# Moving the modulation sums of two output projections to other stages of a two-block network

## The chip, the cores and the metric

One core of a Trainium2 chip. The time is device microseconds of one execution, the median of several runs. The core has five engines that run side by side, each through its own instructions in order: TensorE (PE, with its weight loads as PEld), VectorE (DVE), ScalarE (ACT), GpSimd (POOL) and SyncE (SP), which here issues nearly all DMA transfers.

## The reference, cut to what matters

Two transformer-like blocks run one after the other on x of 1024 tokens by 1024 channels, all in float32. Each block is modulated by six vectors that come from a conditioning vector through a 1024 by 6144 matrix:

```python
mod = (silu(c) @ w_mod + b_mod)                  # block 1; block 2: silu(c_2) @ ada_w + ada_b
sh1, sc1, g1, sh2, sc2, g2 = split(mod, 6)
h = rms(x, norm1_w) * (1 + sc1) + sh1            # block 1's mixers read this
x = x + g1 * (mixed @ w_out)                     # block 1's output projection
h2 = rms(x, norm2_w) * (1 + sc2) + sh2
x = x + g2 * conv_ffn(h2)                        # up projection, convolution, down projection
# block 2 alike, with layer norms and its own mixers; its gate g2 (part 5 of ada_w) is read by its last FFN stage
```

## The kernel before

The program is one class, `Net`; `run` calls the stages in order: `setup`, `block1_in`, `mixers`, `block1_out`, `block1_ffn` (an up stage and a down stage), `block2_in`, `block2_out`, `block2_ffn`. Matrix products are made of three PE passes over float32r halves (high by high, high by low, low by high), so every weight piece of 128x1024 that SP loads into one of two `wr` buffers is split by ACT (the high part) and by POOL or DVE in turn (the low part). In an output projection and a down stage a weight piece is first multiplied by the block's gate row on DVE (lines 134 and 1182).

A vector of the modulation is not a PE product but a sum over eight slabs of 128 rows of its weight: each slab is loaded, and each half (512 columns) is multiplied by the conditioning value of its partition and added to an accumulator. At the end PE adds over the partitions: with four matmuls for each half where a column layout is wanted (`mod_col`, line 208), or with one matmul to a single row (`mod_row`, line 227), to which DVE adds a bias row loaded by SP and which SP then stores to the tensor `gates` in DRAM.

Where these sums stand:
- block 1's `sh1` and `sc1`: in `block1_in`.
- block 1's gate 1 (`mod_gate1`): in `mixers`, whose work is ordered by the string `SSKKKSKKKKKQMSQQQQQAQAQGAAAAAA` (S: a quarter of the S5 layer, K: a tile of keys and values, Q: of queries, M: gate 1, A: attention, G: the gated linear unit). One half is summed by DVE alone (line 248), the other by ACT (product, line 242) and POOL (add, line 244). The slabs use the three buffers `sb`, of which the attention's bias setup holds one first, and the accumulators the two buffers `pp`, which the bias setup uses before.
- block 1's `sh2` and `sc2` (`MODS_OUT`) and block 2's gate of its FFN (`MODS_OUT2`): inside the two output projections, through `mods_out`, a generator from which `out_gemm` takes four steps after each of its first four tiles. A step is one slab of 512 KB into an `xn` buffer and two sums on DVE (lines 278 and 280). The `xn` and `hT` buffers are those of the norm that follows.
- the other sums: in block 1's up stage (`mods_up`) and down stage (`mods_down`), in steps of one half slab (256 KB into one of two `mw` buffers, one DVE sum, lines 299 and 301). The down stage takes three steps for each weight load: one behind the gate product, one behind each of two splits. `mods_end` turns the sums into columns and rows after tile 3 of the second column half, all through one PSUM bank.

The order of instructions on each engine is not the program's alone. A planner goes through the program with its own estimate of each instruction's time and puts on each engine, at each moment, the ready instruction that comes first in the program. What it estimates wrongly shows on the chip as a wait, because every engine's order is then fixed. `behind` only keeps a step's instructions from going ahead of a given one on the same engine.

`out_gemm` runs the projection of eight token tiles in two column halves: the first halves of tiles 0 to 3, their second halves, and then both halves of tiles 4 to 7. The weights of the second half are loaded after tile 1 of the first (`ws.append(load(1))`). `down_proj` runs two column halves over eleven weight loads each, with eight token tiles for each load.

Of the kernel before, what the change touches and what calls it, by code (L numbers as in the profile page):

```python
# [19 lines left out]
F32 = mybir.dt.float32  # L20
# [4 lines left out]
ALU = mybir.AluOpType  # L25
AX = mybir.AxisListType

P = 128
D = 1024
L = 1024  # L30
KT = D // P
# [5 lines left out]
ALPHA = 2.0 ** 0.25  # L37
# [28 lines left out]
class Net:  # L66
# [161 lines left out]
        nc.vector.tensor_add(b, b, ps)  # L228
        nc.sync.dma_start(self.gates[i:i + 1, sl], b)

    def mod_gate1(self, pool):

        nc = self.nc
        accs = [pool.tile([P, 512], F32, tag="pp", name="macc", bufs=2) for _ in range(2)]
        for k in range(KT):
            t = pool.tile([P, D], F32, tag="sb", name="mw", bufs=3)
            nc.sync.dma_start(t, self.a["w_mod"][k * P:(k + 1) * P, 2 * D:3 * D])
            s = self.cact[:, k:k + 1]
            for half, acc in enumerate(accs):
                th = t[:, half * 512:half * 512 + 512]  # L240
                if half:
                    nc.scalar.mul(th if k else acc, th, s)
                    if k:
                        nc.gpsimd.tensor_add(acc, acc, th)
                elif k == 0:
                    nc.vector.tensor_scalar(acc, th, s, None, op0=ALU.mult)
                else:
                    nc.vector.scalar_tensor_tensor(acc, th, s, acc, op0=ALU.mult, op1=ALU.add)
        for half, acc in enumerate(accs):
            self.mod_row(0, half, acc, "bm2", "m")  # L250


    MODS_OUT = [("w_mod", 3, [0], "sh2", "bm3"), ("w_mod", 4, [0], "sc2", "bm4")]
    MODS_UP = [("w_mod", 5, 0, 1, "bm5"), ("ada_w", 0, 1, "sh_a", "ab0"), ("ada_w", 0, 2, "sh_a", "ab0"),
               ("ada_w", 1, 1, "sc_a", "ab1"), ("ada_w", 1, 2, "sc_a", "ab1")]
    MODS_DOWN = [("ada_w", 2, 1, 2, "ab2"), ("ada_w", 3, 1, "sh_b", "ab3"), ("ada_w", 4, 1, "sc_b", "ab4")]
    MODS_OUT2 = [("ada_w", 5, [1], 3, "ab5")]

    def mod_put(self, to, half, acc, bias, vec, role):

        if isinstance(to, int):
# [1 line left out]
        else:  # L263
            self.mod_col(to + ("c" if vec == 2 else ""), half, acc, bias, role, plus_one=to.startswith("sc"),
                         gain="norm2" if to == "sc2" else None)

    def mods_out(self, pool, plan, role):

        nc, v = self.nc, self.nc.vector
        for w, part, (vec,), to, bias in plan:  # L270
            accs = [pool.tile([P, 512], F32, tag="hT", name="macc", bufs=2) for _ in range(2)]
            for k in range(KT):
                t = pool.tile([P, D], F32, tag="xn", name="xn", bufs=4)
                nc.sync.dma_start(t, self.a[w][k * P:(k + 1) * P, part * D:(part + 1) * D])
                for half, acc in enumerate(accs):
                    th, s = t[:, half * 512:half * 512 + 512], self.cact[:, vec * 8 + k:vec * 8 + k + 1]
                    if k == 0:
                        v.tensor_scalar(acc, th, s, None, op0=ALU.mult)
                    else:
                        v.scalar_tensor_tensor(acc, th, s, acc, op0=ALU.mult, op1=ALU.add)  # L280
                if k == KT - 1:
                    for half, acc in enumerate(accs):
                        self.mod_put(to, half, acc, bias, vec, role)
                yield

    def mod_half(self, w, part, vec, half, acc, pool):

# [390 lines left out]
    def mixers(self):  # L678

        nc, v, a = self.nc, self.nc.vector, self.a  # L680
        mq = self.mq
        t2 = lambda r: mq.tile([P, 512], F32, tag="q" + r, name="q" + r, bufs=2)
        self.attn_setup(mq)
        order = "SSKKKSKKKKKQMSQQQQQAQAQGAAAAAA"
        wk = wq = None
        kq = {c: 0 for c in "KQSMAG"}
        old, self.aT = self.aT, []
        qs, st = [], {}
        gl = ExitStack()

        def attend(s):
            if s < 2 * NT:
                self.attn_score(mq, s, qs, st)
            if 0 < s <= 2 * NT:
                self.attn_values(mq, t2, s - 1, st)
            if s > 2 and s % 2:
                self.attn_out(t2, (s - 3) // 2, st)

        ops = False
        for c in order:  # L700
            i = kq[c]
            kq[c] += 1
            if c == "K":
                wk = wk or [self.piece(a["w_kv"][k]) for k in range(2)]
                self.kv_tile(i, wk, t2, old)
            if c == "S":
                self.s5_quarter(i, self.tables)
                if i < 3:
                    self.tables = self.s5_tables(self.s5p, i + 1)
                else:  # L710
                    self.s5ctx.close()
            if c == "M":
                self.mod_gate1(mq)
            if c == "Q":
                wq = wq or [self.piece(a["w_q"][k]) for k in range(4)]
                qs.append(self.q_tile(i, wq, old, t2))
            if c == "A":
                if not ops:
                    ops = True
                    self.psum(1, o=1)  # L720
                if i % 4 == 0 and len(self.aT) == i // 4:
                    self.aT.append(self.new_act())
                attend(2 * i)
                attend(2 * i + 1)
            if c == "G":
                while len(self.aT) < 2:
                    self.aT.append(self.new_act())
                self.glu(self.pool(gl, "m1g", "right"))
        attend(2 * NT)
        attend(2 * NT + 1)  # L730
        gl.close()
        self.m1q.close()
# [210 lines left out]
                hi, lo = (t[:, m].rearrange("p (c t) -> p c t", t=8) for t in self.aT[n])  # L943
                self.split(hi, lo, zv)

    def out_gemm(self, pool, name, gate, xs_in, done, order, alpha=None, step=iter(()), act_in=None):

        nc, v = self.nc, self.nc.vector
        g = self.gate_row(gate)
# [12 lines left out]
        ws = [load(0)]  # L962

        for nh, i in [(0, 0), (0, 1), (0, 2), (0, 3), (1, 0), (1, 1), (1, 2), (1, 3), *((h, i) for i in range(4, NT) for h in (0, 1))]:
# [8 lines left out]
                v.scalar_tensor_tensor(xo, xo, alpha, ps, op0=ALU.mult, op1=ALU.add)  # L973
            if nh:
                done(i)
            elif i < 4:
                for _ in range(4):
                    next(step, None)
                if i == 1:
                    ws.append(load(1))  # L980

    def block1_out(self):
        nc, a = self.nc, self.a
# [21 lines left out]
        def turn(i):  # L1005
            if i % 4 == 0:
                new.append(self.new_act())
            if i % 2:
                self.transpose_mod(xn[i - 1:i + 1], new[-1], self.mods["sc2"], self.mods["sh2"], htile, i % 4 - 1, ("s5", "tp"))

        self.out_gemm(pool, "w_out", 0, lambda i: a["x"][i * P:(i + 1) * P], self.pipe(norm, turn),
                      (4, 5, 6, 7, 0, 1, 2, 3), step=self.mods_out(pool, self.MODS_OUT, "m"))
        self.aT = new
        es.close()

# [148 lines left out]
    def down_proj(self, down, gate, g_dr, x_dr, setup, done, slots, alpha, mods):  # L1164
# [12 lines left out]
        def load(nh, q):  # L1177
# [1 line left out]
            r = self.raw(self.a[down][nh * NQ + q])  # L1179
            w = [self.w.tile([P, 1024], F32R, tag=t, name=t, bufs=4) for t in ("wh", "wl")]  # L1180
            r2 = r.rearrange("p (k n) -> p k n", k=2)
            self.behind(v.tensor_tensor(r2, r2, gh, op=ALU.mult), step)
            self.split_on(nc.gpsimd, *w, r)
            hs = []
            for p in (2 * q, 2 * q + 1):
# [461 lines left out]
    def block2_out(self):  # L1647
# [27 lines left out]
        def turn(i):  # L1675
            if i % 4 == 0:
                new.append(self.new_act())
            if i % 2:
                self.transpose_mod(xn[i - 1:i + 1], new[-1], self.mods["sc_b"], self.mods["sh_b"], htile, i % 4 - 1)

        self.out_gemm(pool, "w_out2", 2, lambda i: None if i < 5 else self.x_dr[i], self.pipe(norm, norm2, turn), (6, 7, 4, 0, 1, 2, 5, 3), ALPHA,
                      self.mods_out(pool, self.MODS_OUT2, "tp"), mix_in)
        self.aT = new
        es.close()
        self.x5.close()
# [135 lines left out]
```

## Time and profile before

| | us |
|---|---|
| median of 3 runs | 2634.54 |
| lowest and highest run | 2631.08 and 2636.38 |
| the profiled execution | 2632.81 |
| its span, first to last instruction | 2630.4 |

The profile comes from that one execution. A busy share is the time in which an engine executed; the chain that ended last follows the end of the program back through what released each step; a wait is the idle time of an engine before an instruction, with the instruction or transfer that ended it. The granted clock is the share of TensorE's full clock in a stretch: 1.00 is 2.4 GHz, and the lower level is 1.2 GHz.

### The profile page before, as it was taken

What the parts mean: (1) busy time and instruction counts of PE and PEld (TensorE: products, weight loads), DVE (VectorE), ACT (ScalarE), POOL (GpSimd) and SP (SyncE); (2) the same over time, 40 slices, a digit from 0 to 9 for tenths busy, and PEclk for the clock granted to TensorE, in tenths of its full rate; (3) what the DMA queues carried; (4) which work ended last, traced back from release to release, by engine and by line L of the source; (5) the groups of instructions that cost most, each with busy time, mean ns of one, the idle gap of its engine ahead of it and who ended that gap; (6) DMA issues with size and microseconds to landing.
All of it is one profiled execution on the core that took longest, in us unless ns stands there. A gap on an engine that the chain in (4) does not pass through costs nothing.

```text
span 2630.4 us, 31222 instructions
## 1 busy us (share of the span) xinstructions
PE 2454.8 (93%) x11558; PEld 1996.0 (76%) x11558; DVE 1816.2 (69%) x2634; ACT 1002.2 (38%) x1473; POOL 1260.8 (48%) x769
## 2 busy tenths in 40 slices
PE   7989998989999989999998889998988999999998
PEld 3867776867788778788787677876766888887886
DVE  7387656588888896655157766678868777778645
ACT  3324462533333333224325545453234333333221
POOL 3253142368888862122125535445255777773222
PEclk8998798999999989999999989998999999999999
DMA  6522116213444348554120101113311222226442
GB/s 242 150 64 56 26 52 236 99 39 132 139 137 140 129 159 295 199 200 154 66 69 27 40 13 53 53 61 125 139 57 56 88 80 89 73 102 263 163 144 88
DMA packets 119015, 295.71 MB, mean 112 GB/s; under 512 B 24144, under 2 KB 38272, under 8 KB 118864
## 3 DMA queue, kind: packets, MB, share of 16 engines
q1 hardware_dynamic: 112528, 270.66, 30.5%
q10 hardware_dynamic: 6336, 23.07, 2.2%
q8 instruction: 91, 1.49, 0.2%
q14 instruction: 60, 0.49, 0.1%
HBM read 243.19 MB, written 49.31 MB: 111 GB/s over the span
## 4 chain that ended last, share of the span: by engine, by line
PE 65%; DVE 16%; DMA 6%; issue 5%; POOL 4%; ACT 4%; SPq 0%; POOLq 0%; ACTq 0%; DVEq 0%
PE ps_d L1199 15%; PE ps_U L1034 13%; PE ps_g L159 7%; PE ps_v L1034 7%; PE ps_Z L159 5%; PE ps_z L159 4%; PE ps_y L1034 3%; PE ps_lv L1593 2%; DVE cv L1262 1%; DMA wr<-in_w_down 1%; PE ps_s L607 1%; DVE wl L142 1%; DMA a<-in_w_mod 1%; PE ps_s L159 1%; DMA wr<-in_w_out 1%
## 5 line engine op out<-in xcount | busy, mean ns | idle before, releaser
L146 POOL TENSOR_TENSOR wl<-wr,wh 128x512 fp32r<-128x512 f32 (+1 forms) x158 | 291.7, 1858 | 446.6 <-ACT wh L145 446.6
L1034 PE MATMUL ps_U<-a,wh 128*128 128x512 f32 x1216 | 375.3, 390 | 3.9 <-DVE cv L1262 2.3
L1199 PE MATMUL ps_d<-wh,gh 128*128 128x512 f32 x704 | 276.3, 393 | 7.8 <-ACT gh L145 4.9
L1199 PE MATMUL ps_d<-wl,gh 128*128 128x512 f32 x704 | 275.7, 392 | 0.0
L1199 PE MATMUL ps_d<-wh,gl 128*128 128x512 f32 x704 | 270.5, 389 | 0.0
L1034 PEld LDWEIGHTS ps_U<-a,wh 128*128 128x128 f32 x1216 | 227.4, 188 | 53.2 <-issue 6.7
L159 PE MATMUL ps_g<-wh,a 128*128 128x512 f32 (+1 forms) x768 | 243.6, 395 | 17.1 <-ACT wh L140 11.7
L1034 PE MATMUL ps_U<-a,wl 128*128 128x512 f32 x608 | 235.8, 390 | 1.5 <-POOL wl L146 1.4
L1281 DVE SCALAR_TENSOR_TENSOR cv<-ps_U,cols,cv 128x945 f32<-128x945 f32 (+2 forms) x176 | 213.5, 1218 | 27.4 <-ACT cv L1273 24.7
L159 PE MATMUL ps_Z<-a,wh 128*128 128x512 f32 x704 | 227.4, 402 | 0.0
L146 POOL TENSOR_TENSOR wl<-S,wh 128x512 fp32r<-128x512 f32 (+1 forms) x114 | 213.3, 1886 | 20.1 <-ACT wh L145 19.4
L145 ACT CAST gh<-rx 128x1024 fp32r<-128x1024 f32 x88 | 89.9, 1047 | 275.1 <-issue 117.4
L159 PEld LDWEIGHTS ps_g<-wh,a 128*128 128x128 f32 x768 | 145.9, 199 | 48.1 <-ACT wh L140 12.6
L1199 PEld LDWEIGHTS ps_d<-wh,gh 128*128 128x128 f32 x704 | 133.0, 189 | 37.8 <-ACT gh L145 4.9
L145 ACT CAST wh<-S 128x512 fp32r<-128x512 f32 (+1 forms) x114 | 84.0, 761 | 202.8 <-POOL S L1114 142.1
L146 DVE TENSOR_TENSOR gl<-rx,gh 128x1024 fp32r<-128x1024 f32 x88 | 126.0, 1453 | 50.2 <-ACT gh L145 50.1
L159 PE MATMUL ps_g<-wl,a 128*128 128x512 f32 (+1 forms) x384 | 150.7, 392 | 5.2 <-POOL wl L142 5.2
L159 PEld LDWEIGHTS ps_Z<-a,wh 128*128 128x128 f32 x704 | 134.9, 194 | 26.5
L1199 PEld LDWEIGHTS ps_d<-wl,gh 128*128 128x128 f32 x704 | 133.0, 189 | 28.1 <-issue 0.9
L142 POOL TENSOR_TENSOR wl<-wr,wh 128x1024 fp32r<-128x1024 f32 x35 | 90.3, 2581 | 133.4 <-ACT wh L140 130.7
L1199 PEld LDWEIGHTS ps_d<-wh,gl 128*128 128x128 f32 x704 | 132.3, 188 | 27.4
L145 ACT CAST wh<-wr 128x512 fp32r<-128x512 f32 (+1 forms) x158 | 112.8, 736 | 91.9 <-PE ps_U L1034 40.2
(526 smaller groups left out, 5856.7 us busy)
## 6 DMA issues: line engine op xcount, KB each, us to landing
mw<-in_ada_w SPq DMA_DIRECT2D x112, 256.0 KB
wr<-in_w_up SPq DMA_DIRECT2D x44, 512.0 KB
rx<-g_w_up SPq DMA_DIRECT2D x44, 512.0 KB
wr<-in_f_up SPq DMA_DIRECT2D x44, 512.0 KB
rx<-g_f_up SPq DMA_DIRECT2D x44, 512.0 KB
g_w_up<-cv ACTq DMA_DIRECT2D x22, 512.0 KB
wr<-in_w_down SPq DMA_DIRECT2D x22, 512.0 KB
g_f_up<-cv ACTq DMA_DIRECT2D x22, 512.0 KB
```

What stands on the lines that cost most here:

```text
L142: (self.nc.gpsimd if self.turn else self.nc.vector).tensor_sub(lo, x, hi.bitcast(F32))
L145: self.nc.scalar.copy(hi, x)
L146: return eng.tensor_sub(lo, x, hi.bitcast(F32))
L159: self.nc.tensor.matmul(out, a, b, start=i == 0, stop=i == n - 1)
L607: nc.tensor.matmul(ps[:, gp, 1:P], wc[o:o + 64, r, gp, 1:9].rearrange("p k h -> p (k h)"), st[o:o + 64, r, gp, 0:P - 1], start=False, stop ...
L1034: self.nc.tensor.matmul(out, a, b, start=start and i == 0, stop=stop and i == 11, skip_group_check=True)
L1199: nc.tensor.matmul(ps, a[:, sl], b, start=q == 0 and j == 0, stop=q == NQ - 1 and j == 5, skip_group_check=True)
L1262: v.scalar_tensor_tensor(t[:, s:], us[part][:, :L - s], wt(j), t[:, s:], op0=ALU.mult, op1=ALU.add)
L1281: v.scalar_tensor_tensor(ov, s[:, r0 + di:r1 + di, c0 + dj:c1 + dj], wt(3 * (di + 1) + dj + 1), ov, op0=ALU.mult, op1=ALU.add)
L1593: nc.tensor.matmul(ps[:, j], ck(kk)[:, j], ck(qq)[:, j], start=True, stop=True)
```

## The change

Block 1's `sh2` and `sc2` move to `mixers`: `mod_gate1` becomes `mod_early`, which takes any entry of a list, and the order string gets two M more at its front. Block 2's FFN gate moves to the list of block 1's down stage, which takes a second step behind each gate product. `mods_out` and the steps in `out_gemm` go.

```diff
-    def mod_gate1(self, pool):
+    def mod_early(self, pool, i):
         nc = self.nc
+        w, part, (vec,), to, bias = self.MODS_OUT[i]
...
-            nc.sync.dma_start(t, self.a["w_mod"][k * P:(k + 1) * P, 2 * D:3 * D])
-            s = self.cact[:, k:k + 1]
+            nc.sync.dma_start(t, self.a[w][k * P:(k + 1) * P, part * D:(part + 1) * D])
+            s = self.cact[:, vec * 8 + k:vec * 8 + k + 1]
...
-            self.mod_row(0, half, acc, "bm2", "m")
+            self.mod_put(to, half, acc, bias, vec, "m")
-    MODS_OUT = [("w_mod", 3, [0], "sh2", "bm3"), ("w_mod", 4, [0], "sc2", "bm4")]
+    MODS_OUT = [("w_mod", 3, [0], "sh2", "bm3"), ("w_mod", 4, [0], "sc2", "bm4"), ("w_mod", 2, [0], 0, "bm2")]
-    MODS_DOWN = [("ada_w", 2, 1, 2, "ab2"), ("ada_w", 3, 1, "sh_b", "ab3"), ("ada_w", 4, 1, "sc_b", "ab4")]
-    MODS_OUT2 = [("ada_w", 5, [1], 3, "ab5")]
+    MODS_DOWN = [("ada_w", 2, 1, 2, "ab2"), ("ada_w", 3, 1, "sh_b", "ab3"), ("ada_w", 4, 1, "sc_b", "ab4"),
+                 ("ada_w", 5, 1, 3, "ab5")]
-    def mods_out(self, pool, plan, role):
...
-        order = "SSKKKSKKKKKQMSQQQQQAQAQGAAAAAA"
+        order = "MMSSKKKSKKKKKQMSQQQQQAQAQGAAAAAA"
...
-                self.mod_gate1(mq)
+                self.mod_early(mq, i)
...
             if nh:
                 done(i)
-            elif i < 4:
-                for _ in range(4):
-                    next(step, None)
-                if i == 1:
-                    ws.append(load(1))
+            elif i == 1:
+                ws.append(load(1))
...
-            self.behind(v.tensor_tensor(r2, r2, gh, op=ALU.mult), step)
+            ins = v.tensor_tensor(r2, r2, gh, op=ALU.mult)
+            self.behind(ins, step)
+            self.behind(ins, step)
```

## Rows read from the trace of the kernel before

**Rows 1.** The page's first part: busy us, share of the span, instructions.
```profile
PE 2454.8 (93%) x11558; PEld 1996.0 (76%) x11558; DVE 1816.2 (69%) x2634; ACT 1002.2 (38%) x1473; POOL 1260.8 (48%) x769
```

**Rows 2.** Stretches: length, busy us and instructions by engine, PE's granted clock, DMA share, GB/s.
```profile
140.00:150.00 10.00, 6.69 (x29) 4.98 (x30) 8.97 (x19) 0.37 (x2) 7.47 (x6) 0.56 0.00 1
145.00:240.00 95.00, 93.94 (x561) 73.90 (x561) 71.21 (x228) 28.76 (x65) 38.66 (x25) 0.98 0.23 50
410.00:440.00 30.00, 20.38 (x67) 15.44 (x67) 15.77 (x19) 5.43 (x7) 6.66 (x5) 0.77 0.82 311
440.00:525.00 85.00, 83.91 (x415) 69.58 (x416) 52.20 (x81) 32.36 (x60) 22.29 (x19) 1.00 0.41 147
1840.00:1845.00 5.00, 3.78 (x17) 2.81 (x15) 0.07 (x1) 0.00 (x0) 0.00 (x0) 1.00 1.03 420
1850.00:1860.00 10.00, 9.79 (x32) 7.89 (x33) 6.63 (x9) 1.05 (x1) 0.15 (x1) 0.72 0.50 185
1860.00:1902.00 42.00, 42.00 (x188) 32.93 (x188) 38.30 (x75) 8.67 (x11) 13.29 (x12) 1.00 0.23 88
```

**Rows 3.** Chain that ended last, block 2's output projection: start us, us, what.
```profile
1820.76 3.52 DMA wr<-in_w_out
...
1835.32 9.81 DMA wr<-in_w_out
...
1860.45 0.95 PE ps_tp L227 x2
```

**Rows 4.** SP's queue, block 2's output projection: start us, us, issues.
```profile
1830.61 1.75 SPq L274 DMA_DIRECT2D xn<-in_ada_w  x4
...
1833.53 0.96 SPq L967 DMA_DIRECT2D xs<-x_dr  x2
```

**Rows 5.** PE in order of time, same place: idle before and what ended it.
```profile
1847.51 1.20 PE L159 MATMUL ps_g<-wh,a 128*128 128x512 f32 x4 [3.74 <-ACT wh L140]
1850.21 0.80 PE L159 MATMUL ps_g<-wl,a 128*128 128x512 f32 x1 [1.49 <-POOL wl L142]
```

**Rows 6.** Instructions on the sums' tiles: ns min/median/max, first and last start.
```profile
L280 DVE SCALAR_TENSOR_TENSOR macc<-xn,cact,macc x42: 737/745/2727, 430.2 to 1856.8; 128x512 f32<-128x512 f32 x42
...
L248 DVE SCALAR_TENSOR_TENSOR macc<-mw,cact,macc x7: 721/751/1778, 121.4 to 142.5; 128x512 f32<-128x512 f32 x7
L244 POOL TENSOR_TENSOR macc<-macc,mw x7: 1277/1300/1637, 123.8 to 139.9; 128x512 f32<-128x512 f32 x7
```

**Rows 7.** Chain that ended last, block 1's output projection.
```profile
429.54 5.66 DMA wr<-in_w_out
...
447.90 0.79 PE ps_m L208 x8
```

**Rows 8.** PE in order of time, block 1's output projection.
```profile
440.10 0.50 PE L159 MATMUL ps_g<-wl,a 128*128 128x512 f32 x1 [1.44 <-POOL wl L142]
```

**Rows 9.** PE in order of time, the mixers: gate 1's row sum.
```profile
143.31 1.87 PE L227 MATMUL ps_m<-macc,ones 128*1 128x512 f32 x2 [7.76 <-DVE macc L248]
```

**Rows 10.** ACT in order of time, block 1's down stage.
```profile
1079.65 1.05 ACT L145 CAST gh<-rx 128x1024 fp32r<-128x1024 f32 x1 [6.08 <-PE ps_d L1199]
...
1090.54 1.05 ACT L145 CAST gh<-rx 128x1024 fp32r<-128x1024 f32 x1 [6.00 <-PE ps_d L1199]
```

**Rows 11.** POOL in order of time, block 1's down stage.
```profile
1095.66 2.45 POOL L146 TENSOR_TENSOR wl<-wr,wh 128x1024 fp32r<-128x1024 f32 x1 [8.60 <-ACT wh L145]
```

**Rows 12.** Chain that ended last, block 1's down stage.
```profile
1081.85 5.96 DMA wr<-in_w_down
...
1093.17 5.35 DMA wr<-in_w_down
```

**Rows 13.** PE in order of time, the turn to the second half.
```profile
1103.87 0.47 PE L1199 MATMUL ps_d<-wh,gh 128*128 128x512 f32 x1 [1.63 <-DVE a L1208]
...
1112.10 0.50 PE L1199 MATMUL ps_d<-wh,gh 128*128 128x512 f32 x1 [1.19 <-DVE xs L1208]
```

**Rows 14.** DVE in order of time, block 1's down stage.
```profile
1094.42 0.75 DVE L301 SCALAR_TENSOR_TENSOR a<-mw,cact,a 128x512 f32<-128x512 f32 x1 [1.69 <-DMA mw<-in_ada_w]
```

More of the change, by code (lines that the diff above doesn't have):

```diff
@@ L265, in mod_put @@
                          gain="norm2" if to == "sc2" else None)
-    def mods_out(self, pool, plan, role):
[L269 to L284, printed above, removed]
     def mod_half(self, w, part, vec, half, acc, pool):
@@ L944, in glu, with out_gemm @@
                 self.split(hi, lo, zv)
-    def out_gemm(self, pool, name, gate, xs_in, done, order, alpha=None, step=iter(()), act_in=None):
+    def out_gemm(self, pool, name, gate, xs_in, done, order, alpha=None, act_in=None):
         nc, v = self.nc, self.nc.vector
@@ L1011, in block1_out @@
         self.out_gemm(pool, "w_out", 0, lambda i: a["x"][i * P:(i + 1) * P], self.pipe(norm, turn),
-                      (4, 5, 6, 7, 0, 1, 2, 3), step=self.mods_out(pool, self.MODS_OUT, "m"))
+                      (4, 5, 6, 7, 0, 1, 2, 3))
         self.aT = new
@@ L1679, in turn @@
                 self.transpose_mod(xn[i - 1:i + 1], new[-1], self.mods["sc_b"], self.mods["sh_b"], htile, i % 4 - 1)
-        self.out_gemm(pool, "w_out2", 2, lambda i: None if i < 5 else self.x_dr[i], self.pipe(norm, norm2, turn), (6, 7, 4, 0, 1, 2, 5, 3), ALPHA,
-                      self.mods_out(pool, self.MODS_OUT2, "tp"), mix_in)
+        self.out_gemm(pool, "w_out2", 2, lambda i: None if i < 5 else self.x_dr[i], self.pipe(norm, norm2, turn), (6, 7, 4, 0, 1, 2, 5, 3), ALPHA, mix_in)
         self.aT = new
```

## The prediction

> **What bounds the kernel now.** I read the page first: TensorE (PE) is busy 93% of the span [rows 1], so what the change is worth is read from the places where PE waits or runs at its lower clock, and what it costs from PE instructions and waits that it adds. Then the table of stretches [rows 2] says where those places are among the stages that the diff touches. In the stretch of block 1's output projection PE works 20.38 of 30 us at a granted clock of 0.77, and then 83.91 of 85: only its beginning is loose. Block 2's projection has a stretch of 9.79 busy us at 0.72 for 32 matmuls, and then 42.00 of 42. The mixers' middle has PE busy 93.94 of 95 us with DVE at 71.21: PE-bound, with 24 us free on DVE. Last I followed the chain that ends last and the PE and SP queues through each place.
>
> **Block 2's projection: what leaves it.** Eight loads of 512 KB, 16 sums on DVE, two row sums on PE. The chain goes through a piece of the projection weight that takes 9.81 us to land, where the piece before it took 3.52 [rows 3]. The SP queue shows why: four loads of the sums (2.1 MB) were issued 4.7 us before it, with two rows and two x tiles behind them [rows 4], and the core's DMA moved 420 GB/s in the 5 us before the landing [rows 2]. PE pays 3.74 + 1.49 us for it [rows 5]. Without the 2.1 MB the piece lands 2.1/0.42 = 5.0 us sooner, at 1840.1 in place of 1845.1. From that landing to PE's first product on the split, at 1850.2, are 5.1 us, so the split would be there at 1845.2; PE was free for the piece at 1847.51 - 3.74 = 1843.8 and has four products of 1.20 us together on its high part first. That leaves a wait of some 0.7 of the 5.23: gain 4.5 (bounds 0, if the two rows and x tiles alone hold it, and 5.2). The wait also costs clock: 32 matmuls in 9.79 us at 0.72 against 188 in 42.00 at 1.00 [rows 2], which would take 7.15: gain 2.6 (bounds 0 and 2.6). The row sums are two pairs of 0.95 us on PE's chain [rows 3]: 1.9. Together 9.0. The 16 sums by 0.75 us [rows 6] leave DVE, which is not what PE waits for in 1860 to 1902; nothing for that.
>
> **Block 1's projection: what leaves it.** Sixteen loads, 32 sums, four column groups. The weight piece at 429.54 lands after 5.66 us [rows 7], 2.1 more than 3.52, with four sum loads ahead of it; PE waits 1.44 for its split [rows 8]. I take the 1.4 as gone (bounds 0 and 1.4). The three longer PE waits before it (xs loads, a POOL split) don't touch the sums and stay. The column groups are 4 by 0.79 us on PE's chain [rows 7]: 3.2. Freed DVE and buffers help nothing: after 440 PE is busy 83.91 of 85 us. Together 4.6.
>
> **Where block 1's sums go.** Two sets of what gate 1 already does in the mixers: each 8 loads, 8 sums on DVE, 8 products on ACT, 7 adds on POOL, then four-column groups. The eight columns a set cost PE the same 3.2 us there, in a PE-bound stretch: loss 3.2. Durations for DVE, POOL and PE are those of gate 1's rows [rows 6, 9]. The 16 DVE sums are about 12 us, the columns 1 more, under DVE's 24 idle us of 145 to 240: no cost if they lie in those gaps, up to 13 if none do. The dear part is a wait. Gate 1's row sum stands in PE's queue ahead of K tiles and waited 7.76 us for the DVE sum before it [rows 9]; the stretch around it ran at 0.56 granted [rows 2]: its 6.69 busy us would be 3.75 at 1.00, and of these 2.9 I count 2, for part of that stretch is the sum's own: about 10 per set. Behind PE's waiting instruction are the key tiles' matmuls; behind the loads that wait for buffers on SP's queue are the S5 reloads, the GLU weights and the next table load. The new sets come first in program order, take gate 1's place behind the bias setup, and gate 1 follows third, since all three use the same two accumulators; that is some 20 us later each, and gate 1's row is read only by weight products after 238 us. Bounds for two more sets: 0 (PE, already late by the first wait, finds the later sums done) and 20 (each waits as gate 1 did). The first wait comes because loads start late behind the bias; the second and third set have their first three loads landed early. I choose 4.
>
> POOL and DVE run side by side here: of gate 1's seven DVE sums the median is 751 ns and the longest 1778; of the seven POOL adds 1300 and 1637 [rows 6]. So one sum in seven is lengthened by 1 us; for 14 adds that is 2 us of DVE time, inside its idle time. The Trainium skill's page "SBUF — State Buffer", section "Who interferes with whom", has a DVE instruction with two SBUF inputs contend with a GpSimd instruction that reads SBUF, the loser blocked for the whole instruction. By that rule at its worst the sum of the kernel's time would be 6 us longer, and it is rival four below; the trace agrees that some are blocked, not that all are.
>
> **Where block 2's sums go.** Block 1's down stage gets a fourth step for each weight load: 16 more loads of 256 KB and 16 more DVE sums by 0.75 us over 17 weight loads (68 steps for 65 needed; before 51 for 49). PE sets the pace there: ACT casts the next activations only when PE frees their buffers, 10.9 us apart [rows 10]. With six such buffers (three weight loads) a load begins two such periods, 21.8 us, before PE needs it, and its split ends 7.6 us after the cast at 1090.54 [rows 11]: 14 us of lead, in which a sum more hides. But SP issues each weight behind sum loads, and the loop from one weight issue to the next is 11.3 us [rows 12], just over PE's pace. One place has no slack: the turn from the first column half to the second, where DVE's accumulations stand behind a gate product that waits for its weight; PE waits 1.63 + 1.19 us [rows 13]. A sum more may lengthen it by one DVE sum or by a load's wait, or the order falls so that it vanishes: bounds -2.8 and +4; I take +1. At the stage's end two more row sums on PE, 1.9 us, in a stretch where PE is never idle: loss 1.9. Their row loads and stores (2 KB) go one after another through SP among x stores that nobody waits for; a DVE add that waits for its row holds up the norm steps behind it, which I leave to the +1's bounds.
>
> **Sum.** Against the profiled execution's 2632.8 us (span 2630.4; the runs' median is 2634.5, 1.7 above it): -9.0 - 4.6 + 3.2 + 4 + 1.9 + 1 = -3.5, so 2629 us. What a measurement of this kernel can tell from no change is about 0.2%, 5.3 us: faster is under 2629.3, slower over 2639.8.
>
> **Rivals.**
> One, the mixers swallow the sums: no wait added, only the 3.2 us of columns. 2632.8 - 13.6 + 3.2 + 1.9 + 1 = 2625. For it: 24 us free on DVE and PE's other tiles; against it: the 7.76 us that one set cost.
> Two, the other side: each new set stalls PE as gate 1's does, 20 us in place of 4: 2645, slower. It decides from 14.5 us on, one and a half such waits. For it: the same helper, the same buffers, and the order of instructions that put a PE row before its sum was done; against it: the later sets' loads are early.
> Three, the SP loop becomes the pace of the down stage. One sum more makes it 12.0 us against 10.9: 17 by 1.1 = 19, less the 14 of lead, +5: 2634. If each weight load also waits for a sum's load, as DVE does for 1.69 us once [rows 14], 17 by 2.8 less 14 is +34: 2663. Against it: the 14 us of lead, and ACT's casts follow PE's buffers, not the loads [rows 10].
> Four, POOL's adds block DVE: 14 by 1.3 us is 18 us of DVE; with the sums' 12 that is 30 against 24 idle, 6 us late: 2635.
>
> **How the numbers follow.** Forecast 0.42; one 0.22, two 0.20, three 0.10, four 0.06. Predicted 2629, its own range 2624 to 2634. For the range: its low end takes rival one with the down stage's turn gone (2625 - 3.8 = 2621) and some of gate 1's own wait (another 4); its high end is rival two's time: 2617 to 2645, leaving out the far end of three and part of two. Faster: one, and half of the forecast, 0.41. Slower: most of two and of three, 0.27. The same: the rest, 0.32.
>
> **What would show it.** In the profile after: the weight pieces at block 2's second half land in 4 to 5 us, and PE's 3.7 us wait before the last pieces is gone (right) or names another load (wrong). In the mixers, PE's waits at the column groups and the row, together: about 12 us with gate 1's own for the forecast, 8 for rival one, 24 or more for two. In the down stage PE stays whole but at the turn; a wait for weights at any other tile is rival three. The prediction is wrong if the sets before the mixers delay the S5 chain, so that attention starts late without any PE wait at a sum, or if the changed order of instructions opens a wait in a stage that the diff doesn't touch.

## The result and the profile after

The changed kernel takes 2644.89 us (median of 12 runs, 2637.35 to 2660.73), the kernel before 2628.91 us in the 12 runs beside it (2615.80 to 2639.86). The ratio is 1.0066, with a 95% interval of 1.0040 to 1.0091: slower by 17 us (10.5 to 24). The sum of the forecast was 3.5 us faster, 2629 us.

The runs of one kernel spread over more than 20 us, so the two profiled executions (2632.81 and 2658.69 us) are not the medians, and the first thing to ask of their difference is what of it belongs to the change. I cut both traces at the same places in the program: the attention's last value product, the down stage's first product, the first and the last intra-block product of block 2's scan, and the last `ps_v` product (high T3 by high weight) of block 2's up stage. These are the stretches of the kernel before, in the view of rows 2: from 95 us to the end of the attention; block 1's projection and up stage; the down stage to the scan's start; block 2's projection and up stage; and last the 50 us that will matter in the mixers.

```profile
95.00:408.90 313.90, 293.41 (x1638) 232.03 (x1637) 202.67 (x569) 138.34 (x325) 119.76 (x85) 0.88 0.25 67
408.90:979.80 570.90, 535.49 (x2371) 435.55 (x2370) 454.49 (x431) 214.37 (x291) 395.22 (x226) 0.97 0.39 135
979.80:1415.70 435.90, 426.30 (x1936) 349.61 (x1936) 234.13 (x366) 151.67 (x190) 115.03 (x62) 0.99 0.45 158
1802.80:2365.90 563.10, 530.23 (x2304) 428.99 (x2303) 424.23 (x467) 194.77 (x264) 344.70 (x237) 0.97 0.26 91
155.00:205.00 50.00, 50.00 (x295) 38.94 (x296) 36.20 (x97) 12.28 (x23) 20.27 (x15) 1.00 0.26 64
```

The same stretches of the changed kernel:

```profile
95.00:426.80 331.80, 303.58 (x1651) 239.46 (x1650) 226.27 (x593) 144.52 (x338) 137.29 (x99) 0.85 0.30 85
426.80:996.00 569.20, 534.00 (x2338) 435.06 (x2337) 433.16 (x390) 214.76 (x291) 393.19 (x226) 0.97 0.36 121
996.00:1449.00 453.00, 431.19 (x1939) 351.27 (x1939) 252.11 (x383) 151.84 (x190) 114.61 (x62) 0.97 0.47 161
1834.80:2392.20 557.40, 525.76 (x2301) 427.87 (x2300) 415.20 (x449) 194.95 (x264) 350.28 (x237) 0.97 0.24 84
155.00:205.00 50.00, 44.39 (x253) 34.39 (x252) 48.68 (x106) 17.71 (x32) 33.27 (x22) 1.00 0.52 155
```

The mixers got 18 us longer, the down stage 17, block 2's projection 6 shorter, block 1's 2. Length less PE's busy time is PE's idle time: 20.5 us before and 28.2 after in the mixers, 9.6 and 21.8 in the down stage. Where means over executions are given further down, the one of `e5` is left out as slow (2672.99 us, over 1.5% above that kernel's fastest run).

**The mixers.** PE in order of time in the changed kernel; the last number is the wait before, with what ended it:

```profile
138.38 1.87 PE L208 MATMUL ps_m<-ones,macc 128*128 128x1 f32 x8 [7.76 <-DVE macc L249]
...
168.45 1.02 PE L208 MATMUL ps_m<-ones,macc 128*128 128x1 f32 x8 [1.63 <-DVE macc L249]
...
196.25 0.63 PE L760 MATMUL ps_tp<-ident,qn 128*128 128x128 f32 x4 [1.96 <-DVE qn L754]
...
201.03 1.02 PE L227 MATMUL ps_m<-macc,ones 128*1 128x512 f32 x2 [1.37 <-DVE macc L249]
...
259.83 0.79 PE L808 MATMUL ps_g<-kT,q 64*128 64x256 f32 x1 [5.90 <-DVE mx L812]
```

The first set's columns wait exactly as long as gate 1's row did [rows 9], and the two later sets wait 1.63 and 1.37 us. The sums' waits are 10.8 us together, near the 12 that the prediction named for its forecast. But PE also waits for a query's norm and for an attention maximum, which no sum touches; the longest such waits before were 0.2 and 0.9 us. Each of them waits for DVE, and the fifth row of the windows points to why: DVE is busy 48.68 of 50 us from 155 to 205 us, where it was 36.20, and PE falls from 50.00 to 44.39. The attention's first score product starts at 217.8 us in place of 210.7.

**The down stage.** In order of time in the changed kernel: PE at the turn; SP's weight issues ahead of it, with a group of four sum loads; and DVE's waits in the loop.

```profile
1133.13 0.77 PE L1179 MATMUL ps_d<-wh,gh 128*128 128x512 f32 x1 [14.52 <-DVE a L1188]
```

```profile
1062.96 0.38 SPq L121 DMA_DIRECT2D wr<-in_w_down  x1
1063.48 10.29 SPq L272 DMA_DIRECT2D mw<-in_ada_w  x4
...
1077.55 0.42 SPq L121 DMA_DIRECT2D wr<-in_w_down  x1
...
1092.79 0.42 SPq L121 DMA_DIRECT2D wr<-in_w_down  x1
...
1106.80 0.38 SPq L121 DMA_DIRECT2D wr<-in_w_down  x1
...
1120.34 0.38 SPq L121 DMA_DIRECT2D wr<-in_w_down  x1
```

```profile
1097.81 2.06 DVE L282 SCALAR_TENSOR_TENSOR a<-mw,cact,a 128x512 f32<-128x512 f32 x2 [5.44 <-DMA mw<-in_ada_w]
...
1108.72 0.75 DVE L282 SCALAR_TENSOR_TENSOR a<-mw,cact,a 128x512 f32<-128x512 f32 x1 [2.37 <-DMA mw<-in_ada_w]
...
1113.07 0.49 DVE L280 TENSOR_SCALAR a<-mw,cact 128x512 f32<-128x512 f32 x1 [3.60 <-DMA mw<-in_ada_w]
1114.41 1.23 DVE L1160 TENSOR_TENSOR wr<-wr,grow 128x1024 f32<-128x1024 f32 x1 [0.86 <-DMA wr<-in_w_down]
```

From the first of these weight issues to the fifth are 57.4 us, 14.3 for each loop, where PE needs a weight every 10.9 [rows 10] and the same four loops before took 11.8 on average (issues at 1045.81 and 1093.17; the 11.3 of [rows 12] is the last of them). The loop is a circle: a sum's load cannot be issued before the sum two ahead of it has freed one of two buffers, the next weight stands behind that load in SP's queue, and the next sums and the gate product stand behind the late sum in DVE's. DVE is not short of time in the circle, it waits for loads. The lead is spent by the end of the first half, and PE waits 14.52 us at the turn, for an accumulation that stands in DVE's queue behind sums that wait and late splits. Behind the turn the loop falls to 12.6 us (11.6 before), and no wait of PE in the second half is longer than 0.27.

**Block 2's projection.** The weight pieces of the chain that ended last, and PE's waits in front of the projection's last pieces:

```profile
1853.12 3.50 DMA wr<-in_w_out
...
1867.69 5.98 DMA wr<-in_w_out
```

```profile
1864.14 1.26 PE L159 MATMUL ps_g<-wh,a 128*128 128x512 f32 x4 [3.92 <-ACT wh L140]
1866.63 0.80 PE L159 MATMUL ps_g<-wl,a 128*128 128x512 f32 x1 [1.23 <-POOL wl L142]
1878.60 0.50 PE L159 MATMUL ps_g<-wl,a 128*128 128x512 f32 x1 [1.02 <-POOL wl L142]
```

The piece that took 9.81 us [rows 3] takes 5.98 (4 to 5 were forecast), and the wait of 3.74 before the last pieces [rows 5] is gone; 1.02 on a split is left of it.

### The profile page after: what moved, and what is told of

Read it like the earlier page. It is cut to its first block, busy times and chain, and to the rows that moved or that the text cites. A ratio compares the mean times of both kernels' runs of the same rounds, so it can differ in the third digit from the quotient of the medians.

```text
span 2656.9 us, 31271 instructions
## 1 busy us (share of the span) xinstructions
PE 2461.4 (93%) x11558; PEld 2005.4 (75%) x11558; DVE 1825.5 (69%) x2618; ACT 1008.8 (38%) x1486; POOL 1282.7 (48%) x783
## 3 DMA queue, kind: packets, MB, share of 16 engines
q8 instruction: 91, 1.49, 0.2%
## 4 chain that ended last, share of the span: by engine, by line
PE 63%; DVE 19%; DMA 7%; issue 5%; ACT 3%; POOL 3%; SPq 0%; POOLq 0%; DVEq 0%; ACTq 0%
PE ps_U L1012 13%; PE ps_d L1179 13%; PE ps_g L159 7%; PE ps_v L1012 6%; PE ps_Z L159 5%; PE ps_z L159 4%; PE ps_y L1012 3%; DMA mw<-in_ada_w 3%; PE ps_lv L1573 2%; DVE cv L1242 1%; DVE cv L1261 1%; PE ps_g L808 1%; DVE gl L146 1%; PE ps_s L588 1%; PE ps_o L844 1%
## 5 line engine op out<-in xcount | busy, mean ns | idle before, releaser
L159 PE MATMUL ps_g<-wh,a 128*128 128x512 f32 (+1 forms) x768 | 240.8, 393 | 14.3 <-ACT wh L140 7.9
L146 POOL TENSOR_TENSOR wl<-S,wh 128x512 fp32r<-128x512 f32 (+1 forms) x114 | 213.5, 1887 | 15.0 <-ACT wh L145 14.3
L1570 POOL TENSOR_TENSOR qq<-qq,q 128x512 f32<-128x512 f32 x56 | 79.1, 1417 | 140.7 <-ACT qq L1569 140.7
```

What stands on the lines that cost most here:

```text
L146: return eng.tensor_sub(lo, x, hi.bitcast(F32))
L159: self.nc.tensor.matmul(out, a, b, start=i == 0, stop=i == n - 1)
L1570: g.tensor_tensor(qq, qq, qn, op=ALU.mult)
```

## The experiments

Theory A after the first look: two places cost, each by itself, the mixers through DVE and the down stage through the loads' circle. Rivals: only one of them costs, and the other belongs to the one profiled execution.

**One part at a time.** `e1`: block 1's part alone (the new order and `mod_early`; block 2's gate stays in block 2's projection). `e2`: block 2's part alone:

```diff
-    MODS_DOWN = [("ada_w", 2, 1, 2, "ab2"), ("ada_w", 3, 1, "sh_b", "ab3"), ("ada_w", 4, 1, "sc_b", "ab4")]
-    MODS_OUT2 = [("ada_w", 5, [1], 3, "ab5")]
+    MODS_DOWN = [("ada_w", 2, 1, 2, "ab2"), ("ada_w", 3, 1, "sh_b", "ab3"), ("ada_w", 4, 1, "sc_b", "ab4"),
+                 ("ada_w", 5, 1, 3, "ab5")]
+    MODS_OUT2 = []
-            self.behind(v.tensor_tensor(r2, r2, gh, op=ALU.mult), step)
+            ins = v.tensor_tensor(r2, r2, gh, op=ALU.mult)
+            self.behind(ins, step)
+            self.behind(ins, step)
```

> Block 1's part alone: its two sets stand ahead of the mixers, block 2's gate stays in block 2's projection. Theory A (each move costs by itself: DVE becomes the pace of the mixers, and DVE's wait for sum loads the pace of the down stage): the mixers end 18 us later and block 1's projection gives back 2, so +16 us, ratio 1.006. Theory B (only the down stage costs, and the mixers' delay belongs to the one profiled execution): 0 or -2 us, ratio 0.999 to 1.000. Theory C (only the mixers cost): +16 us as under A, with the next kernel telling them apart.

> Block 2's part alone: its gate's sums are the fourth step of block 1's down stage, the mixers and block 1's projection as before. Theory A: +17 us at the turn of the down stage with a PE wait of 10 to 15 us there, -6 in block 2's projection, so +11 us, ratio 1.004. Theory B: the same +11. Theory C: the down stage's 14.5 us wait belongs to the one profiled execution; -6 to -9 us, ratio 0.997.

`e1`: ratio 1.0050 (1.0026 to 1.0073), slower by 13 us, 16 expected. `e2`: 0.9998 (0.9971 to 1.0025), where 1.004 was expected, which lies outside; but its trace has the wait at the turn again, and the stage is 455.9 us long:

```profile
1106.33 0.76 PE L1202 MATMUL ps_d<-wh,gh 128*128 128x512 f32 x1 [18.17 <-DVE a L1211]
```

So the down stage's wait is no accident of one execution, and the mixers' loss is there without it: theory A. That `e2` ends level all the same is partly its gain in block 2's projection; the rest is taken up below.

**The circle of the loads.** `e3` is the changed kernel with four load buffers in the down stage, and each load issued three sums ahead:

```diff
-                yield from self.mod_half(w, part, vec, half, acc, pool)
+                jobs += [(w, part, vec, half, acc, k) for k in range(KT)]
...
+                tiles.append(pool.tile([P, 512], F32, tag="mw", name="mw", bufs=4))
...
+        for j in range(3):
+            load(j)
+        for j, (w, part, vec, half, acc, k) in enumerate(jobs):
+            yield
...
+            load(j + 3)
```

> The changed kernel, with four buffers in place of two for the loads of the down stage's sums and each load issued three sums ahead. If DVE's wait for a sum's load, which two buffers let start only after the sum two before, makes the loop of 14 us: the weight issues come 11 us apart again, PE's 14.5 us wait at the turn falls under 3, and the time is 12 us below the changed kernel, ratio to the kernel before 1.002 to 1.003. If the transfers themselves are the pace (1 MB of sums beside 1.5 MB of weight and activations for each weight load): the loop stays at 13 to 14 us, the wait stays, ratio 1.006 as the changed kernel.

Ratio 0.9987 (0.9964 to 1.0010), some 21 us below the changed kernel's; 12 were expected. The down stage and PE at the turn:

```profile
983.30:1419.60 436.30, 426.91 (x1939) 348.73 (x1940) 249.52 (x383) 151.28 (x190) 114.62 (x62) 0.99 0.48 167
```

```profile
1107.16 0.47 PE L1198 MATMUL ps_d<-wh,gh 128*128 128x512 f32 x1 [1.33 <-DVE a L1207]
...
1115.69 0.50 PE L1198 MATMUL ps_d<-wh,gh 128*128 128x512 f32 x1 [1.42 <-DVE xs L1207]
```

The same 64 sums and the same bytes take 436.3 us in place of 453.0, and the turn waits 1.33 and 1.42 us, much as in the kernel before [rows 13]. The transfers (0.48 of the DMA engines' time) and DVE (249.52 of 436.30 us) were not the limit; the two buffers were, with the single load ahead that they allow.

Two more kernels check it. `b1` is `e2` with the four buffers, `h4` the kernel before with them and nothing moved. (Every kernel with four buffers also has a constant tile narrowed from 32 to 16 columns, and the stage's last norm, which shares the buffers, gets two more.)

> Block 2's part alone, with four buffers for the down stage's sum loads. Theory A (two buffers made the turn's wait): PE's wait at the turn under 3 us as in the kernel before, block 2's projection 4 to 6 us shorter, so -3 to -5 us, ratio 0.998 to 0.999, and 15 us or more below the same kernel with two buffers in the stage from the first product of the down stage to block 2's scan. Theory B (the run time of the kernel with block 2's part alone, no different from before, says that the turn's wait is paid back elsewhere): the same time as with two buffers, ratio 1.000.

> The kernel before with four load buffers in the down stage and nothing moved. If the gain of the version with block 2's part alone and four buffers (0.9937) is that of the emptied projection with the down stage unharmed: this one gains only what is left of the turn's 1 to 6 us wait, ratio 0.998 to 1.000. If it is the buffers' own: ratio 0.994 to 0.996.

`b1`: 0.9937 (0.9913 to 0.9962), below what either theory gave. `h4`: 0.9976 (0.9952 to 1.0000), near the 0.998 to 1.000 expected if only the turn's wait goes. The length of the down stage over all kernels: three steps with two buffers 435.9 to 440.0 us (4 executions), four with two 449.3 to 455.9 (5), four with four 436.3 to 438.4 (5), three with four 432.6 and 432.7 (2). The fourth step with two buffers stands alone; with four buffers it lies where three steps with two lie. The part behind the last product, where the norm runs, is no shorter with four buffers (means 185.8 against 186.0 us with four steps, 184.0 against 184.1 with three), so the norm's two buffers do not make the difference.

**What costs in the mixers.** Six kernels leave out work of block 1's two new sets. `g1`, `g2` and `g3` are the changed kernel: `g1` without 14 of the 16 DVE sums, `g2` without the 14 POOL adds, `g3` with one slab loaded for each set. `h1`, `h2` and `h3` are `e3` without the DVE sums, without the POOL adds, and without both. The edit of `h3`, of which `h1` has the first part and `h2` the second:

```diff
             for half, acc in enumerate(accs):
+                if half == 0 and k and i < 2:
+                    continue
...
-                    if k:
+                    if k and i == 2:
                         nc.gpsimd.tensor_add(acc, acc, th)
```

> The changed kernel with 14 of the 16 DVE sums of the two new sets left out (loads, ACT products, POOL adds and columns stay). Read at the start of the first score product, which lay at 203.8 to 210.7 us in three executions of the kernels with the old mixers and at 216.6 to 219.8 in three with the new. If DVE's time is what delays it: 206 to 210. If the loads or POOL's adds: 215 or later.

> The changed kernel with the 14 POOL adds of the two new sets left out (loads, ACT products, DVE sums and columns stay). If POOL's adds block DVE or S5's own POOL work: the first score product at 210 or earlier. If DVE's time or the loads: 215 or later.

> The changed kernel with one slab loaded for each new set in place of eight; all sums, products and adds stay and read that slab. If the wait for slabs delays the mixers: the first score product at 210 or earlier and PE's waits at the columns under 3 us. If the engines' work: 215 or later.

> The changed kernel with four load buffers in the down stage (ratio 0.9987 as it stands), and 14 of the 16 DVE sums of the two new sets left out. If DVE's time for the sums is the mixers' loss: the time falls by 8 to 10 us, ratio 0.995 to 0.996. If POOL's adds or what the sets do to the order of instructions: within 3 us, ratio 0.998 to 0.999.

> The same with the 14 POOL adds of the two new sets left out in place of the DVE sums. If POOL's adds hold up DVE's and POOL's own work for the S5 layer: 8 to 10 us less than the full version, ratio 0.995 to 0.996, and DVE's 40 us of unbroken work from 155 to 205 us gets gaps. If DVE's own sums are the loss: ratio 0.998 to 0.999.

> The same with both left out, DVE sums and POOL adds (loads, ACT products and PE columns stay). If the engines' work on the sums is the mixers' loss: 10 to 13 us less than the full version, ratio 0.994 to 0.995. If loads, columns and the changed order make it: under 4 us less, ratio 0.997 to 0.999.

`g1` to `g3` ran once each (2643.90, 2635.78 and 2646.47 us). Their first score product started at 216.7, 215.5 and 219.2 us: no single part brings it back. That was a poor thing to read, since another order of instructions puts other PE work in front of it. The ratios were `h1` 0.9971 (0.9954 to 0.9988), `h2` 0.9970 (0.9952 to 0.9988), `h3` 0.9991 (0.9968 to 1.0013), none of which differs clearly from `e3`'s 0.9987; if the engines' work were the loss, 0.995 to 0.996 were expected of the first two and 0.994 to 0.995 of `h3`. What does separate the kernels are two columns of the windows from 95 us to the attention's end, PE's idle time (length less busy) and DVE's busy time. First the kernels with all the work, the changed one above and `e1`:

```profile
95.00:414.60 319.60, 288.60 (x1658) 229.03 (x1656) 225.57 (x593) 145.89 (x339) 137.99 (x99) 0.90 0.32 90
```

Then `h1`, `h2` and `h3`:

```profile
95.00:410.90 315.90, 292.43 (x1650) 234.47 (x1648) 215.53 (x579) 143.87 (x337) 137.58 (x99) 0.87 0.32 89
```

```profile
95.00:416.10 321.10, 301.45 (x1653) 237.33 (x1651) 215.49 (x593) 145.27 (x338) 124.01 (x85) 0.85 0.32 89
```

```profile
95.00:420.70 325.70, 307.71 (x1661) 244.57 (x1659) 210.32 (x579) 146.34 (x339) 120.39 (x85) 0.85 0.32 89
```

| mixers | executions | PE idle, us | DVE busy, us |
|---|---|---|---|
| as before the change | 6 | 14.7 to 20.5, mean 17.6 | 201 to 205, mean 203 |
| both new sets | 3 | 28.2, 31.0, 33.8 | 226, 226, 226 |
| without DVE's sums (`g1`, `h1`) | 2 | 24.2, 23.5 | 219, 216 |
| without POOL's adds (`g2`, `h2`) | 2 | 19.6, 19.7 | 215, 215 |
| without both (`h3`) | 1 | 18.0 | 210 |
| one slab a set (`g3`) | 1 | 24.3 | 227 |

Two sets add 23 us to DVE's busy time, though their sums are 14 of 0.75 us and two of 0.49: 11.5. Taking away POOL's 14 adds, which DVE does not execute, takes 11 us off DVE's busy time (7 where DVE's sums are out too, against the mean of `g1` and `h1`) and 11 of the 13 us off PE's idle time. DVE's instructions last longer beside the adds, by 0.8 us on average for each add of 1.3. The traces show that this is where the time goes. Take for each kind of DVE instruction its median where no POOL instruction overlaps it. Above that, DVE's instructions in the mixers last 29 to 32 us in sum in the six executions with the mixers of before, 44 with both new sets, and 31 without POOL's new adds. The instructions that overlap no POOL work come to within 0.7 us of nothing in each, so all of it lies beside POOL's work.

The adds are not the whole loss, though. `g3` has all of DVE's work (227 us) but loads one slab a set, and PE idles 24.3 us in place of 28 or more. From one execution that is a hint, not a proof, that waiting for slabs costs too.

The total time does not follow these columns in the ratios; the clock moves it by more. `e2` and `b1` have the same PE instructions in the same order from end to end, and the mixers of the kernel before. Their attention, from the first score product to the last value product:

```profile
206.10:393.80 187.70, 176.58 (x1006) 138.86 (x1005) 131.63 (x412) 106.06 (x261) 68.60 (x50) 0.89 0.17 42
```

```profile
204.40:416.60 212.20, 205.61 (x1006) 160.07 (x1005) 132.71 (x412) 105.97 (x261) 68.64 (x50) 0.75 0.15 37
```

The same 1006 matmuls take 187.7 us at a granted clock of 0.89 and 212.2 at 0.75. These 24.5 us are as much as a kernel's runs differ by, and more than anything that the sums can do there. (The two ran on different chips, but the six runs of `b1`, on one chip, spread by 24 us too, at mean clocks from 0.949 to 0.959.)

The clock can be taken out in part, since every run of an experiment has its mean granted clock on record. Within the kernels the time falls by 2.0 us for each 0.001 of it (1.6 to 2.8 kernel by kernel, correlations -0.87 to -1.00). Brought to 0.954 by that slope, an estimate, `e3` comes to 1.5 us above the kernel before in the runs beside it, and `h1`, `h2` and `h3` to 10.7, 8.9 and 6.9 below: 8 to 12 us less than `e3`, near the size that was expected of leaving out the engines' work. Which of the two sums makes it, this does not tell, since the parts do not add up.

**Other places for the sums.** `b3` has block 1's sets as half slabs behind the attention's steps, with two load buffers and an accumulator of their own, all on DVE. `e5` and `b2` are the kernel before with block 2's gate in block 2's own up stage, one sum behind every sixth step (`e5`) or every third (`b2`):

```diff
-                       self.mods_out(pool, self.MODS_OUT2, "tp"), mix_in)
+                       act_in=mix_in)
...
-                 (2, 3, 4, 5, 6, 7, 0, 1), alpha=ALPHA)
+                 (2, 3, 4, 5, 6, 7, 0, 1), self.spread(self.mods_up("y", self.MODS_UP2), 6), alpha=ALPHA, end_up=self.m2.close)
```

> Block 1's part alone, with its two sets not ahead of the mixers but in half slabs behind the attention's steps, with two load buffers and an accumulator of their own, all sums on DVE. Theory A (ahead of the mixers DVE is the pace, in the attention it has idle time): the first score product starts at 204 to 211 us as in the kernel before, the attention is not longer but for 3 us of columns, block 1's projection keeps its gain of 2 to 7, so -1 to -4 us, ratio 0.9985 to 0.9995. Theory D (each set costs wherever it stands, by PE's waits at its columns): +5 to +10 us, ratio 1.002 to 1.004.

> The kernel before, with block 2's gate sums taken out of block 2's projection and put into block 2's own up stage, one sum behind every sixth step. Nothing else moves. If the gain of the emptied projection is real and needs only a stage that hides 16 sums: -6 us (what the trace of the changed kernel shows there) to -9 (the prediction's sum), ratio 0.9965 to 0.998. If DVE, busy 70 to 80% there, is the pace of that stage: 12 us of sums come back, ratio 1.001 to 1.002.

> Block 2's gate in block 2's own up stage, one sum behind every third step in place of every sixth, so that the row is stored near the middle of that stage. If the 19.5 us wait at the start of block 2's down stage came from the late gate row alone: the wait is gone, the stretch from block 2's scan to the end of its up stage stays 9 us shorter than before, and the ratio is 0.9965 (-9 us). If DVE is the pace of that up stage: the wait goes, but the stage gets up to 12 us longer, ratio 1.000 to 1.001.

`b3`: 1.0200 (1.0162 to 1.0238), some 53 us, far past both theories. The waits by engine and line, DVE's two largest between 200 and 480 us (us in total, times, longest):

```profile
DVE macc L300 <- DMA mw<-in_w_mod: 22.8, 1, 22.8
DVE macc L302 <- DMA mw<-in_w_mod: 17.2, 13, 6.9
```

A sum put into DVE's queue before its slab has landed holds the attention's work behind it for 22.8 us. Neither theory had the load in it. How much of the 53 us these waits make was not separated: PE idles 47.8 us in the mixers (17.6 in the mean before), and the attention also ran at a granted clock of 0.69.

`e5`: 1.0050 (1.0026 to 1.0074), where 0.9965 to 0.998 was expected. In its profiled execution the up stage is as short as hoped (554.0 us from the scan's end); then PE stands still at the start of the down stage, and SP's queue shows that the gate row was stored and read back only there:

```profile
2415.53 2.93 PE L1205 MATMUL ps_d<-wh,gh 128*128 128x512 f32 x6 [19.47 <-ACT wh L145]
```

```profile
2397.59 0.29 SPq L229 DMA_DIRECT2D gates<-mrow  x1
...
2404.65 0.63 SPq L150 DMA_DIRECT2D grow<-gates  x1
```

The sums, spread over too many steps, ended at 2391 us. `b2` takes them earlier: ratio 0.9974 (0.9949 to 0.9999), the wait gone, 556.4 us, near the expected 0.9965.

`b4` joins the two edits that gained, four buffers in the down stage and the gate in block 2's up stage.

> The kernel before with two edits: block 2's gate in block 2's own up stage (one sum behind every third step), and four load buffers in the down stage, which keeps its three steps. If the two gains are separate (0.9974 and 0.9976 by themselves): -13 us, ratio 0.995, with the down stage 432 to 433 us long and the stretch from block 2's scan to the end of its up stage 554 to 557. If the single ratios were mostly the granted clock of their runs: 0.997 to 0.999.

0.9926 (0.9895 to 0.9958), 19.5 us faster than before, 7 runs. It has the lowest ratio here, though not clear of `b1`'s, and is faster than both kernels of the study. The two stages in its trace, at their expected lengths:

```profile
974.20:1406.90 432.70, 425.80 (x1935) 349.79 (x1936) 234.72 (x365) 151.60 (x190) 113.67 (x62) 0.99 0.46 159
1793.60:2350.30 556.70, 526.52 (x2304) 426.57 (x2303) 429.31 (x467) 193.54 (x264) 358.44 (x237) 0.97 0.27 92
```

## Why the prediction was wrong

The direction was wrong: two terms of the sum were mis-sized, and they are the two in which moved work arrives: the +1 for the turn of the down stage, and the +4 for the mixers with its DVE work at nothing. Where several executions share a stage, means are compared. The second row leaves out `b3` and `g3`, whose stage is shorter (560.4 and 558.4 us) for a reason that was not looked for; with them it would be -5.6.

| term | predicted, us | measured, us |
|---|---|---|
| block 2's projection emptied | -9.0 | -6.6 (564.0, 4 executions, to 557.4, 10) |
| block 1's projection emptied | -4.6 | -3.9 (571.8, 6 executions, to 567.9, 8) |
| mixers, columns | +3.2 | +4.8 busy (1.87, 0.95, 1.02 and 0.95) |
| mixers, waits | +4 | +13.4 of PE idle time (17.6, 6 executions, to 31.0, 3) |
| down stage, first half and turn | +1 | +9.8 (127.0, 4 executions, to 136.7, 5) |
| down stage, second half | 0 | +1.8 (127.7 to 129.5) |
| down stage, rows behind the last product | +1.9 | +1.9 (184.1 to 186.0) |

The down stage is +13.5 together (438.8 to 452.3). With the columns at the forecast's 3.2, as in the sums below, all add up to +19.6, against a measured 17 (10.5 to 24).

**The turn of the down stage is the step that failed most.** The prediction took +1 for it, with +4 as its bound, and put the loop of the loads among the rivals at 0.10, with 12.0 us for the loop or 13.7 if each weight load also waits once for a sum's load. It measured 14.3 ahead of the turn and 12.6 behind it, since more than one of the four sums waits. The prediction's "14 us of lead" was not there to be used up to its last microsecond over 17 loads: PE meets it at the turn, after the first half's nine. The argument against that rival, that ACT's casts follow PE's buffers and not the loads, was read from a loop of 11.3 us beside PE's 10.9: that row showed a stage that already stood at its limit. `e3` and the stage lengths of all kernels settle this one.

**The mixers.** The waits at the sums were right (10.8 us, 12 forecast; rival two wanted 24 or more). What was missing is what DVE does besides: the prediction set 13 us of DVE work against 24 idle us and called it free, and 2 us for what POOL's adds take from DVE. The trace says 23 us, 7 to 11 of them through POOL's adds. The 2 us came from the sums' own longest times, while the adds lengthen all of DVE's work beside them: already in the kernel before, the 17 DVE instructions that overlap gate 1's seven adds last 4.9 us longer than their kinds do alone. Rival four, given 0.06 and 2635 us, named the mechanism; the 7 to 11 us lie between its 18 and the forecast's 2. Its rule was that of the Trainium skill's page "SBUF — State Buffer", section "Who interferes with whom", that a DVE instruction with two SBUF inputs and a GpSimd instruction reading SBUF contend and the loser waits; the 11 us that go when the adds go agree with it in kind, by 0.8 us of a 1.3 us add on average and not the whole. The gaps of DVE were also in the wrong place: from 155 to 205 us it had 14 idle us of 50, and that is where the work fell. The prediction's sign of being wrong, an attention that starts late without a wait at a sum, came in part: it starts 7 us late, and only 3.0 us of that are waits at sums beyond the 7.76 of before.

**Block 2's projection.** The waiting went as forecast in kind: 1.02 us is left of the 3.74 and 1.49. Against that the split wait at the piece before rose from 0.40 to 1.23 us, so the waits give 3.4, where 4.5 was taken. The two row sums' 1.9 fits the rest. The 2.6 us for the clock did not come: a stretch of 10 us at 0.70 is still there, now behind the wait of 3.92 us that both kernels have.

```profile
1866.00:1876.00 10.00, 9.37 (x30) 7.57 (x31) 3.88 (x3) 0.98 (x1) 0.58 (x1) 0.70 0.81 325
```

**Block 1's projection** was right in size within 1 us (-3.9 for -4.6), columns and the weight piece's wait together.

**What stays open.** Added up by stages, `e1`, `h4`, `b2` and `b4` come out within their intervals (+12.7, -6.1, -7.6 and -13.4 us for 13, -6, -7 and -19.5 measured). `e2`, `e3` and `b1`, which all have the gate's sums in the down stage, should be +6.9, +4.5 and -8.2, and their ratios say -0.5, -3.4 and -16.6: 7 to 8 us better each, just past their intervals. The changed kernel, which has them there too, does not show it. The profiles don't say where this comes from. Brought to one clock as above, the three come to +2.1, +1.5 and -9.2 us, which leaves 4.8, 3.0 and 1.0 of the difference: the clock of the runs is most of it in `e3` and `b1` and a third in `e2`. The same estimate puts `e1` at +8.8 and the changed kernel at about +11 (against the kernel before in the later batches, since the 12 runs beside it have no clock on record), below the +12.7 and +19.6 of the stages. A clock that falls because PE idles is taken out with the rest, so these may be too low. `h4` and `b4` stay where their stages put them (-5.9 and -13.1). Nor do the ratios show that the mixers lose through DVE: leaving out sums gave PE's idle time back, and `h3` with the least idle time is not faster than `e3`; only at one clock is it, by 8 us. Its attention ran at a lower clock in the profiled execution, as the 0.85 of its window shows against the 0.90 of `e1`; whether idle time that is won there is always lost to the clock was not tried.

## What to carry to other kernels

Moved work is not priced by the idle time of the engine that takes it, but by the queue that it stands in: an instruction whose data are late holds everything behind it on its engine, as the 14.5 us at the turn, the 22.8 us in the attention and the 19.5 us behind a late gate row show. Before adding a step to a loop, compare the loop's period with the pace of the engine that sets the time (11.3 against 10.9 us here), and count the buffers: two more of 256 KB brought a stage with a fourth step back to its old length (437.2 against 438.8 us; with three steps they gave 432.7). When one profiled execution differs from another, cut both at the same instructions and ask of each stretch whether kernels that are identical there differ as much.

## What was not expected of the hardware

The granted clock in the attention varies with nothing in PE's instructions to tell why: 0.89 and 0.75 for the same 1006 matmuls in the same order, 187.7 and 212.2 us. And POOL's adds cost DVE time in sum (7 to 11 us for 14 adds) with almost nothing to see in the median DVE instruction beside them. These are the sums of the changed kernel's three sets, ns least, median and longest:

```profile
L249 DVE SCALAR_TENSOR_TENSOR macc<-mw,cact,macc x21: 719/747/2737, 117.0 to 200.3; 128x512 f32<-128x512 f32 x21
L245 POOL TENSOR_TENSOR macc<-macc,mw x21: 1263/1317/2232, 119.4 to 198.1; 128x512 f32<-128x512 f32 x21
```

The median is 747 ns, as 751 was in gate 1's set alone [rows 6]. The longest, 2737 ns, tells little by itself, since 2727 stands in [rows 6] for the output projections; only the sum over all DVE instructions beside the adds shows the cost.
